# Two blocks of the residual stream kept turned for the queries, and a gate's sums moved into the first FFN

## The chip, the cores and the metric

The kernel runs on one core of one Trainium2 chip. The metric is the time of one execution on the device, in microseconds (us). The engines are named as in the profile: PE (TensorE, matrix products and transposes; PEld its weight loads), DVE (VectorE), ACT (ScalarE), POOL (GpSimd) and SP (SyncE, which here only issues DMAs). Each engine works through its own queue in order; a queue's order is fixed when the program is built.

## What is computed

A decoder trunk of two layers on 256 tokens of width 2048, in float32. Layer 0 mixes by causal pooling, layer 1 by latent attention with 16 heads; each layer ends in a SwiGLU FFN of width 5632. Shifts, scales and gates come from a vector c (`sc = silu(c)`).

```python
for i in range(DEPTH):
    shift_m, scale_m, gate_m, shift_f, scale_f, gate_f = jnp.split(sc @ mod_w[i] + mod_b[i], N_MOD, axis=-1)
    if i == N_A:
        kv_shift, kv_scale = jnp.split(sc @ kv_mod_w + kv_mod_b, 2, axis=-1)
        h_kv = modulate(rmsnorm(x, kv_in_norm), kv_shift, kv_scale)
        kv = shared_kv(h_kv, w_dkv, kv_norm, w_uk, w_uv, w_kr, cos, sin)
    h = modulate(rmsnorm(x, norm_mix[i]), shift_m, scale_m)
    if i < N_A:
        y = pool_mixer(h, pool_w[i], pool_scale[i])
    else:
        j = i - N_A
        y = mla_mixer(h, kv, w_dq[j], q_norm[j], w_uq[j], w_o[j], cos, sin)
    x = x + gate_m[:, None, :] * y
    h = modulate(rmsnorm(x, norm_ffn[i]), shift_f, scale_f)
    x = x + gate_f[:, None, :] * swiglu(h, ffn_gate[i], ffn_up[i], ffn_down[i])
return rmsnorm(x, final_norm)
```

The keys and the queries of layer 1 both start from `rmsnorm(x)` of the same x. They differ only in gain, shift and scale per column, so the stream divided by its root mean square and turned (columns to partitions) serves both.

## The kernel before

**Weight units.** Every large product is made of weight units: 512 rows by 512 columns of a weight, 1 MB, loaded by SP into one of six `raw` tiles (`w_unit`, load at L387). ACT rounds it to a high half (L374), DVE subtracts to get the low half (L376), both in tiles `hl` (six, so three units). PE then makes 24 products per unit for the two token tiles (L398): high by high, high by low of the activations, low by high. Activations in halves lie in `act` tiles, eight of 8 KB per partition, which serve many other uses too.

**Background units.** The modulation vectors `sc @ mod_w` are not made on PE, apart from the first ones. Each is a list of units; one unit (`Part.unit`) loads 1 MB of the transposed weight by SP (L210) into a `raw` tile and lets DVE multiply it by `silu(c)` and sum along the row (L211, one instruction that takes the sum along). There are 168, in this order: 24 for the first FFN's shift and scale, 16 for its gate, 32 for the keys' shift and scale, 48 for the attention's shift, scale and gate (`mla`), 32 for the last FFN's shift and scale, 16 for its gate. They are spread by hand: `plan(left, units)` sets a rate so that `left` remain after so many weight units; each `split` of a weight calls `tick`, which issues the units that have come due. `hold` stops this, `release` starts it again with a new rate. In the first FFN the rate is 75 units over 95 weight units, 6 remain for the keys, and 19 lie beside the queries' latent and the heads.

**Stages.** Pooling mixer; first FFN (its first three blocks of 512 columns by `start_ffn`, which pumps eight units in each, then chunks `p`, `t`, `d` in a fixed list); handover into the keys' latent; keys and values (four groups of four heads) with the queries' latent between them; heads in eight pairs; output product with w_o; last FFN; final norm.

**Handover.** `then_attention` runs with its order written by hand on PE, ACT and DVE. While the FFN's last column ends for token tile 0 and then 1, the first two blocks of the stream are scaled (`scale`, L476: block 0 on DVE, block 1 on POOL), turned by PE (`turn`, L482), and made into halves: `upper` (ACT, L490), `whole` (L497 on DVE or L499 on ACT) and `lower` (DVE, L503). Products are L407; `a` is block 0, `b` block 1, the digit the token tile, and the index 0, 1, 2 the group high-high, low-high, high-low. Blocks 2 and 3 follow in a loop: scaled by POOL (L528), turned (L540), halves at L1183 to L1193, products at L1197. Then the rotary key (L1201, L1208) and the latent's norm (L1238 to L1241).

**Queries.** `hidden_q` scales a block again on ACT (`scaled`, L530), turns it with eight transposes (L540), and modulates it (L558 to L560), for each of four blocks.

**Heads.** `project_heads` makes q for a pair (weights split at L1362 and L1363, products L1368 to L1370 and L1288), `probabilities` the softmax (L1383 to L1401), `turned` transposes (L1407), `weighted` the sums over values (L1414, L1415). PSUM has eight banks.

Of the kernel before, what the change touches and what calls it, by code (L numbers as in the profile page):

```python
# [17 lines left out]
P = 128  # L18
# [42 lines left out]
BEGUN = 6  # L61
ASIDE = 5

FFN0_UNITS, MLA_UNITS, HEAD_UNITS, WO_UNITS, FFN1_UNITS = 95, 4, 16, 8, 60

KNOWN = (1, 3, 5, 7, 9, 10, 11, 12)


LATE, MLA_LATE, WO_LATE = 3, 5, 3

V_C, V_NM, V_NF, V_KVIN, V_KVN, V_QN, V_PS, V_B, V_KB, V_END = 0, 16, 48, 80, 96, 100, 104, 120, 312, 344

# [21 lines left out]
def tile_trunk(ctx: ExitStack, tc: tile.TileContext, a: dict, out: bass.AP):  # L94
# [22 lines left out]
    def t2k(shape, dt=F32):  # L117
        return work.tile(shape, dt, tag="t2k", bufs=7, name=nm("t2k"))
# [323 lines left out]
    def run(*lists):  # L442
        for fs in lists:
            for f in fs:
                f()
# [3 lines left out]
    class Handover:  # L449
# [23 lines left out]

        def scale(self, tok, j):
            self.turned[tok, j] = t2k([P, CH]), ps_t().rearrange("p (k t) -> p k t", k=KL), t2k([P, KL, P])
            (dve if j == 0 else pool).tensor_scalar(out=self.turned[tok, j][0], in0=x[:, tok, j * CH:(j + 1) * CH],  # L476
                                                    scalar1=self.rstd[:, tok:tok + 1], scalar2=None, op0=ALU.mult)

        def turn(self, tok, j):
            xr, pt, _ = self.turned[tok, j]  # L480
# [233 lines left out]
    def ffn(l, hT, gate_name, begun, then):  # L714
# [23 lines left out]
        def down(i):  # L738
# [6 lines left out]
            for j in range(ND):  # L745
                js = slice(j * CH, (j + 1) * CH)
                banks = [ps_t() for _ in range(NT)]
                if last and j == ND - 1:
                    hold()
                if last and j == ND - 1:  # L750
                    weights = [w_unit(wd[c, j]) for c in g]
# [118 lines left out]
    def start_ffn(l, first, ahead, hidden, late):  # L870

        begun = begin(l, range(BEGUN), (0,))
        hT = [first(begun[0])] if l == DEPTH - 1 else [first]
        with tc.issue_after(mod_ins[0].ins), tc.issue_after(hid_ins[0].ins) if hid_ins[0] else nullcontext():
            for j in range(ND - 1):
                if l == 0 and j == 1:
                    for tok in range(NT):
                        sync.dma_start(aside[0][:, tok], back[tok])
                todo = KD // 2 if j + 1 >= ND - late else 0
                for n, (c, which) in enumerate((c, w) for c in begun for w in (GATE, UP)):  # L880
                    if n == 2 * len(begun) - 1:
                        hT.append(hidden(j + 1, pieces))
                    if l == 0 or j > 0 or c > 0:
                        begun[c][which].block(j, hT[j])
                    if n == 2 * len(begun) - 5:
                        pieces = ahead(j + 1)
                    if todo:
                        pump(1)
                        todo -= 1
                pump(todo)  # L890
        return hT, begun
# [215 lines left out]
    for j in range(ND):  # L1107
        sf_block(1, j, C_SF1, C_AF1)
    mod_part(1, 5, gate_to, "ffn1")
    n_ffn1, n_blocks, n_mix = KD, KD // 2, KD  # L1110
    n_late = n_ffn1 + LATE * n_blocks
    n_all = n_ffn1 + ND * n_blocks + n_mix

    hT, begun = start_ffn(0, first, hidden_T, lambda j, parts: halves_T(j, parts), ND - 1)
    plan(n_all + MLA_LATE, FFN0_UNITS)

    hkv, rstd, ckv = None, None, []

    def dkv(j):
        return a["w_dkv"][j, 0]  # L1120
# [1 line left out]
    def then_attention(old, banks, piece):  # L1122
# [4 lines left out]
        hkv, rstd = h.hT, h.rstd  # L1127
        w = [w_load_of(dkv(j)) for j in range(2)]
        split_upper(w[0])
        run(h.old(0))  # L1130
        h.start()
        h.piece(0)
# [1 line left out]
        split_upper(w[1])  # L1134
        h.scale(0, 0)
        h.scale(0, 1)
        split_lower(w[0])
        fs = h.old(1)
        run(fs[:-KL])
        h.turn(0, 0)  # L1140
# [22 lines left out]
        h.lower(0, 1)  # L1163
        h.turn(1, 1)
        h.upper(1, 1)
        run(b0[2], a1[2], b1[0], b1[1])
        h.whole(1, 1, dve)
        h.lower(1, 1)
        run(b1[2])

        pieces = [scaled(rstd, j, pool) for j in range(2, ND)]
        for j in range(2, ND):
            w_ = w_load_of(dkv(j))
            if j == 2:
# [3 lines left out]
            split_upper(w_)  # L1178
            t_ = act_t([P, 2, KL, T])
            full = [t2k([P, 2, T]) for _ in range(2)]  # L1180
            columns = [[cols[:, i, j * KL + k:j * KL + k + 1] for i in (C_AKV, C_SKV)] for k in range(KL)]
            for k, (by, plus) in enumerate(columns):
                act.activation(t_[:, 0, k, :], pts[k // 2][:, k % 2, :], AF.Identity, scale=by, bias=plus)  # L1183
            split_lower(w_)
            for k, (by, plus) in enumerate(columns):
                src, dst = pts[k // 2][:, k % 2, :], full[k // 2][:, k % 2, :]
                if k < 2:
                    dve.tensor_scalar(out=dst, in0=src, scalar1=by, scalar2=plus, op0=ALU.mult, op1=ALU.add)
                else:
                    act.activation(dst, src, AF.Identity, scale=by, bias=plus)  # L1190
            for k2 in range(2):
                ks = slice(2 * k2, 2 * k2 + 2)
                dve.tensor_tensor(out=t_[:, 1, ks], in0=full[k2], in1=t_[:, 0, ks].bitcast(F32), op=ALU.subtract)  # L1193
# [103 lines left out]

    def hidden_q():
        nonlocal pieces
        pts = turned_pieces(pieces)  # L1300
        if len(hmx) < ND - 1:
            pieces = scaled(rstd, len(hmx) + 1)
        hmx.append(modulated(pts, len(hmx), C_AM1, C_SM1))

# [10 lines left out]
    pool.memset(krT, 0.0)  # L1315
    rope_end(kr_t, [(slice(0, ROPE), krT[0:ROPE, 0, :]), (slice(ROPE, P), krT[ROPE:P, 1, :])])

    plan(n_all - n_mix - WO_LATE, HEAD_UNITS)
    cq = [ps_t() for _ in range(NT)]
    for j in range(ND):  # L1320
        if len(hmx) < ND:
# [108 lines left out]
    pairs = H // HG  # L1430

    act.activation(small([P, 1]), ones[:, 0:1], AF.Exp)
    hold()
    heads = [project_heads(g) for g in range(2)]
    for o in heads:
        o.finish()
    release(n_all - n_mix - WO_LATE, HEAD_UNITS - 8)

    w_o, ob = a["w_o"], []

# [137 lines left out]
```

## Time and profile before

| | us |
|---|---|
| median of 3 runs | 1918.96 (1916.93 to 1919.68) |
| the profiled execution | 1918.19 |
| its span, first to last instruction | 1916.4 |
| PE busy | 1862.8 (97%) |
| DVE busy | 1402.7 (73%) |
| ACT busy | 850.2 (44%) |
| POOL busy | 26.9 (1%) |
| DMA | 574.98 MB, mean 300 GB/s |

The times of single instructions come from the profiled execution. In the profile's rows a name such as `ps<-hl,act` gives output and inputs without buffer numbers, `x24` a count, and a bracket such as `[0.80 <-POOL t2k L476]` the time for which the engine stood idle just before and the instruction that ended it. The granted clock over the whole span was 0.987 of full speed.

### The profile page before, as it was taken

What the parts mean: (1) busy time and instruction counts of PE and PEld (TensorE: products, weight loads), DVE (VectorE), ACT (ScalarE), POOL (GpSimd) and SP (SyncE); (2) the same over time, 40 slices, a digit from 0 to 9 for tenths busy, and PEclk for the clock granted to TensorE, in tenths of its full rate; (3) what the DMA queues carried; (4) which work ended last, traced back from release to release, by engine and by line L of the source; (5) the groups of instructions that cost most, each with busy time, mean ns of one, the idle gap of its engine ahead of it and who ended that gap; (6) DMA issues with size and microseconds to landing.
All of it is one profiled execution on the core that took longest, in us unless ns stands there. A gap on an engine that the chain in (4) does not pass through costs nothing.

```text
span 1916.4 us, 21930 instructions
## 1 busy us (share of the span) xinstructions
PE 1862.8 (97%) x8813; PEld 1507.8 (79%) x8813; DVE 1402.7 (73%) x1391; ACT 850.2 (44%) x958; POOL 26.9 (1%) x32
## 2 busy tenths in 40 slices
PE   7689999999999999999999999999999999999998
PEld 3255888888888888887889888888888888888887
DVE  2148799999788777799899966889785556645556
ACT  3125643444433334244678745634444433343343
POOL 0000000000000000002100000000000000000000
PEclk9789999999999999999999999999999999999999
DMA  9999998879998888897597775988776666665651
GB/s 399 398 418 417 368 364 333 319 299 361 357 344 332 327 330 326 332 373 274 212 371 291 293 278 194 397 318 335 260 284 240 241 240 239 249 222 205 220 198 44
DMA packets 86647, 574.98 MB, mean 300 GB/s; under 512 B 10977, under 2 KB 15505, under 8 KB 18321
## 3 DMA queue, kind: packets, MB, share of 16 engines
q1 hardware_dynamic: 86018, 570.42, 77.8%
q0 software_dynamic: 432, 3.15, 0.4%
q8 instruction: 69, 1.13, 0.2%
q14 instruction: 32, 0.26, 0.0%
q10 hardware_dynamic: 96, 0.02, 0.0%
HBM read 567.24 MB, written 6.32 MB: 299 GB/s over the span
## 4 chain that ended last, share of the span: by engine, by line
PE 69%; issue 22%; DMA 3%; DVE 3%; ACT 1%; SPq 0%; POOL 0%; POOLq 0%; DVEq 0%; ACTq 0%
PE ps L398 58%; DMA raw<-in_mod_w_dram 3%; PE ps L256 2%; PE ps L973 2%; PE ps L407 2%; PE ps L1288 2%; DVE raw L211 1%; PE ps L729 1%; PE ps L1197 1%; PE ps L540 0%; DMA raw<-in_mod_block_dram 0%; PE ps L196 0%; PE ps L948 0%; PE ps L770 0%; DVE hl L376 0%
## 5 line engine op out<-in xcount | busy, mean ns | idle before, releaser
L398 PE MATMUL ps<-hl,act 128*128 128x512 f32 x6744 | 1539.5, 390 | 1.9 <-DVE hl L376 1.0
L398 PEld LDWEIGHTS ps<-hl,act 128*128 128x128 f32 x6744 | 1263.0, 188 | 264.7 <-DVE hl L376 1.8
L376 DVE TENSOR_TENSOR hl<-raw,hl 128x2048 fp32r<-128x2048 f32 x289 | 661.1, 2289 | 253.2 <-ACT hl L374 252.5
L374 ACT ACTIVATE hl<-raw 128x2048 fp32r<-128x2048 f32 x289 | 553.1, 1918 | 647.8 <-PE ps L398 572.1
L211 DVE SCALAR_TENSOR_TENSOR raw<-raw,s_row 128x2048 f32<-128x2048 f32 x168 | 383.2, 2284 | 3.6 <-DMA raw<-in_mod_wt_dram 3.6
L256 PE MATMUL ps<-raw,s_strip 128*32 128x512 f32 x392 | 65.2, 760 | 34.6 <-DMA raw<-in_mod_w_dram 33.5
L698 DVE TENSOR_TENSOR act<-ps,act 128x512 f32<-128x512 f32 x96 | 64.5, 685 | 17.5 <-PE ps L398 17.5
L256 PEld LDWEIGHTS ps<-raw,s_strip 128*32 128x32 f32 x392 | 9.5, 121 | 70.0 <-DMA raw<-in_mod_w_dram 46.3
L784 DVE TENSOR_TENSOR x<-ps,x 128x512 f32<-128x512 f32 x32 | 22.1, 690 | 38.8 <-PE ps L398 38.8
L1288 PE MATMUL ps<-act,hl 128*128 128x256 f32 x384 | 49.6, 287 | 0.0
L1288 PEld LDWEIGHTS ps<-act,hl 128*128 128x128 f32 x384 | 48.3, 195 | 0.7 <-DVE act L1253 0.2
L407 PE MATMUL ps<-hl,act 128*128 128x512 f32 x192 | 47.0, 400 | 1.2 <-DVE act L503 1.2
L732 ACT ACTIVATE act<-ps 128x512 fp32r<-128x512 f32 x44 | 23.6, 594 | 50.0 <-PE ps L729 37.6
L407 PEld LDWEIGHTS ps<-hl,act 128*128 128x128 f32 x192 | 35.2, 188 | 10.7 <-ACT act L490 2.3
L263 DVE COPY t2k<-ps 128x256 f32<-128x256 f32 x4 | 1.7, 425 | 52.9 <-ACT t2k L262 52.9
L427 ACT ACTIVATE junk<-x 128x512 bf16<-128x512 f32 x23 | 14.5, 629 | 53.2 <-DVE x L612 37.6
L802 DVE TENSOR_TENSOR t2k<-ps,t2k 128x512 f32<-128x512 f32 x24 | 16.5, 689 | 28.5 <-PE ps L398 28.5
L798 ACT ACTIVATE t2k<-ps 128x512 f32<-128x512 f32 x24 | 14.2, 590 | 47.9 <-PE ps L398 47.9
L973 PEld LDWEIGHTS ps<-act,act 128*128 128x128 f32 x128 | 24.7, 200 | 11.6 <-issue 8.4
L696 ACT ACTIVATE act<-ps 128x512 f32<-128x512 f32 x32 | 19.1, 597 | 29.0 <-PE ps L398 28.8
L973 PE MATMUL ps<-act,act 128*128 128x256 f32 x128 | 31.9, 402 | 0.0
L733 DVE TENSOR_TENSOR act<-ps,act 128x512 fp32r<-128x512 f32 x44 | 28.1, 683 | 0.9 <-ACT act L732 0.9
(222 smaller groups left out, 911.6 us busy)
## 6 DMA issues: line engine op xcount, KB each, us to landing
raw<-in_mod_wt_dram SPq DMA_DIRECT2D x136, 1024.0 KB, 5.8
raw<-in_ffn_gate_dram SPq DMA_DIRECT2D x88, 1024.0 KB, 5.8
raw<-in_ffn_up_dram SPq DMA_DIRECT2D x88, 1024.0 KB, 5.1
raw<-in_ffn_down_dram SPq DMA_DIRECT2D x88, 1024.0 KB, 5.2
raw<-in_mod_w_dram SPq DMA_DIRECT2D x48, 1024.0 KB, 12.1
raw<-in_kv_mod_wt_dram SPq DMA_DIRECT2D x32, 1024.0 KB, 7.1
raw<-in_w_o_dram SPq DMA_DIRECT2D x16, 1024.0 KB, 6.1
raw<-in_mod_block_dram SPq DMA_DIRECT2D x8, 1024.0 KB, 12.5
```

What stands on the lines that cost most here:

```text
L211: dve.scalar_tensor_tensor(out=r, in0=r, scalar=1.0, in1=s_row, op0=ALU.mult, op1=ALU.mult, accum_out=self.sums[:, self.n:self.n + 1])
L256: pe.matmul(self.bank[m * STRIP:(m + 1) * STRIP, :], lhsT=weights(k), rhs=r[:, k, i, :], start=first, stop=last)
L374: hi_ins = act.activation(hi, r, AF.Copy)
L376: lo_ins = dve.tensor_tensor(out=lo, in0=r, in1=hi.bitcast(F32), op=ALU.subtract)
L398: pe.matmul(banks[tok], lhsT=t_[:, i, k, tok * P:(tok + 1) * P], rhs=w[:, k, :], start=first and n < len(part), stop=last and n >= len(ord ...
L407: pe.matmul(bank, lhsT=t_[:, i, k, tok * P:(tok + 1) * P], rhs=w[:, k, :], start=first and n == 0, stop=last and n == len(order) - 1)
L698: dve.tensor_tensor(out=part, in0=banks[tok], in1=part, op=ALU.add)
L732: act.activation(m[:, 0, :, ts_], v, AF.Copy)
L733: dve.tensor_tensor(out=m[:, 1, :, ts_], in0=v, in1=m[:, 0, :, ts_].bitcast(F32), op=ALU.subtract)
L784: dve.tensor_tensor(out=x[:, tok, js], in0=banks[tok], in1=x[:, tok, js], op=ALU.add)
L973: pe.matmul(mixed[g][:, n % 2, :], lhsT=wp[g][:, k, ns], rhs=pool_all[g // 2][:, g % 2, k, :], start=k == 0, stop=k == KL - 1)
L1288: pe.matmul(pt[:, h, :], lhsT=w(h0 + h, k), rhs=t_[:, i, k, :], start=n == 0, stop=n == 3 * KL - 1)
```

## The change

Four things are moved:

1. *Kept blocks.* In the keys' latent, blocks 2 and 3 of the stream, turned and not yet modulated, are copied by ACT out of PSUM into a float32 tile of the `act` kind (two copies of 128x512 per block). `hidden_q` takes them from there for its blocks 2 and 3 and no longer scales and turns them.
2. *The gate's units.* `n_mix` goes out of the counts: the 16 units of `mla`'s gate come due before the heads. The first FFN's rate becomes 91 units over 94 weight units. The plans and the hold and release around the heads go; the output product takes eight units over nine weight units in place of five over eight. In the last group of an FFN's down product `hold` comes one column of 512 earlier, which leaves seven units for the keys.
3. *Handover.* `scale` is always on DVE; the low half of the first weight is subtracted ahead of the old products; `a1[2]` goes ahead of `b0[2]`.
4. *Start of an FFN.* In its first block the eight units start at the third weight unit and not at the first.

```diff
-FFN0_UNITS, MLA_UNITS, HEAD_UNITS, WO_UNITS, FFN1_UNITS = 95, 4, 16, 8, 60
+FFN0_UNITS, MLA_UNITS, WO_UNITS, FFN1_UNITS = 94, 4, 9, 60
-LATE, MLA_LATE, WO_LATE = 3, 5, 3
+LATE, MLA_LATE = 3, 5
...
-            (dve if j == 0 else pool).tensor_scalar(out=self.turned[tok, j][0], in0=x[:, tok, j * CH:(j + 1) * CH],
-                                                    scalar1=self.rstd[:, tok:tok + 1], scalar2=None, op0=ALU.mult)
+            dve.tensor_scalar(out=self.turned[tok, j][0], in0=x[:, tok, j * CH:(j + 1) * CH],
+                              scalar1=self.rstd[:, tok:tok + 1], scalar2=None, op0=ALU.mult)
...
-                if last and j == ND - 1:
+                if last and j == ND - 2:
                     hold()
...
-                    if todo:
+                    if todo and (j > 0 or n + 2 >= 2 * len(begun) - todo):
                         pump(1)
...
-    n_ffn1, n_blocks, n_mix = KD, KD // 2, KD
+    n_ffn1, n_blocks = KD, KD // 2
     n_late = n_ffn1 + LATE * n_blocks
-    n_all = n_ffn1 + ND * n_blocks + n_mix
+    n_all = n_ffn1 + ND * n_blocks
...
         split_upper(w[0])
+        split_lower(w[0])
         run(h.old(0))
...
         h.scale(0, 1)
-        split_lower(w[0])
...
-        run(b0[2], a1[2], b1[0], b1[1])
+        run(a1[2], b0[2], b1[0], b1[1])
...
+        mem = act_t([P, 2, KL, T], F32)
+        both = [mem[:, i] for i in range(2)]
...
+            kept.append([both[j - 2][:, 2 * h2:2 * h2 + 2] for h2 in range(2)])
...
+            for pt, dst in zip(pts, kept[-1]):
+                act.activation(dst, pt, AF.Copy)
...
-        pts = turned_pieces(pieces)
-        if len(hmx) < ND - 1:
+        pts = turned_pieces(pieces) if len(hmx) < 2 else kept[len(hmx) - 2]
+        if len(hmx) < 1:
             pieces = scaled(rstd, len(hmx) + 1)
...
-    plan(n_all - n_mix - WO_LATE, HEAD_UNITS)
...
-    hold()
     heads = [project_heads(g) for g in range(2)]
     for o in heads:
         o.finish()
-    release(n_all - n_mix - WO_LATE, HEAD_UNITS - 8)
```

More of the change, by code (lines that the diff above doesn't have):

```diff
@@ L1109, in tile_trunk @@
     mod_part(1, 5, gate_to, "ffn1")
-    n_ffn1, n_blocks, n_mix = KD, KD // 2, KD
+    n_ffn1, n_blocks = KD, KD // 2
     n_late = n_ffn1 + LATE * n_blocks
-    n_all = n_ffn1 + ND * n_blocks + n_mix
+    n_all = n_ffn1 + ND * n_blocks
     hT, begun = start_ffn(0, first, hidden_T, lambda j, parts: halves_T(j, parts), ND - 1)
     plan(n_all + MLA_LATE, FFN0_UNITS)
-    hkv, rstd, ckv = None, None, []
+    hkv, rstd, ckv, kept = None, None, [], []
     def dkv(j):
```

## The prediction

> **What bounds the kernel now.** I read the page first, then stretches of time, then the order of time on single engines where TensorE (PE) waits. In the page's first and fifth parts (line, engine, operation, shapes, count | busy us, mean ns | idle before) the reader is to see that PE is busy 97% of the span, and what one background unit costs on VectorE (DVE): L211, 2284 ns, plus an 83 ns read of its accumulator, together 2.37 us. A weight unit costs DVE 2289 ns (L376).
>
> ```profile
> PE 1862.8 (97%) x8813; PEld 1507.8 (79%) x8813; DVE 1402.7 (73%) x1391; ACT 850.2 (44%) x958; POOL 26.9 (1%) x32
> ...
> L376 DVE TENSOR_TENSOR hl<-raw,hl 128x2048 fp32r<-128x2048 f32 x289 | 661.1, 2289 | 253.2 <-ACT hl L374 252.5
> ...
> L211 DVE SCALAR_TENSOR_TENSOR raw<-raw,s_row 128x2048 f32<-128x2048 f32 x168 | 383.2, 2284 | 3.6 <-DMA raw<-in_mod_wt_dram 3.6
> ```
>
> Busy is not proof of full rate, so I price a matmul by the chain that ended last (start, length, what): 65.08 / 287 = 0.2268 us per 512-column product, 24 of them 5.44 us per weight unit.
>
> ```profile
> 966.98 0.87 PE ps L540 x8
> ...
> 1098.00 65.08 PE ps L398 x287
> ```
>
> Next the stretches (columns: stretch, length, busy time of PE, weight load, DVE, ACT, POOL with counts, PE clock, DMA share, GB/s).
>
> ```profile
> 390.00:885.00 495.00, 494.85 (x2225) 410.44 (x2224) 407.77 (x326) 196.04 (x147) 0.70 (x1) 1.00 0.88 337
> 810.00:890.00 80.00, 79.85 (x361) 66.14 (x360) 74.70 (x68) 33.93 (x31) 0.00 (x0) 1.00 0.91 359
> 810.00:830.00 20.00, 20.00 (x90) 16.56 (x89) 19.30 (x17) 7.91 (x5) 0.00 (x0) 1.00 1.01 420
> ...
> 390.00:450.00 60.00, 60.00 (x274) 49.86 (x273) 59.06 (x58) 27.69 (x27) 0.00 (x0) 1.00 0.78 287
> ...
> 1010.00:1098.00 88.00, 85.59 (x581) 79.18 (x580) 84.76 (x175) 71.31 (x186) 0.61 (x1) 0.98 0.78 286
> 1030.00:1040.00 10.00, 9.19 (x59) 8.99 (x60) 9.12 (x23) 7.79 (x23) 0.00 (x0) 0.83 0.80 289
> 1098.00:1163.00 65.00, 65.00 (x288) 53.79 (x288) 42.85 (x35) 27.40 (x25) 0.00 (x0) 1.00 0.72 270
> ```
>
> The first FFN (390 to 885) holds PE at 494.85 of 495; DVE has 87 us free there, but only 0.94 in 390 to 450 and 5.3 in 810 to 890. In the heads (1010 to 1098) DVE is the fullest, 84.76 of 88. That invites the conclusion that taking units out of the heads gives back their whole DVE time. PE's order of time there says otherwise:
>
> ```profile
> 1010.16 0.28 PE L1368 MATMUL ps<-act,hl 128*128 128x256 f32 x1
> ...
> 1030.81 0.55 PE L1407 MATMUL ps<-con,t2k 128*128 128x128 f32 x3 [1.97 <-ACT t2k L1400]
> 1031.11 0.36 PE L1368 MATMUL ps<-act,hl 128*128 128x256 f32 x1
> ...
> 1033.33 3.81 PE L1288 MATMUL ps<-act,hl 128*128 128x256 f32 x24
> 1036.98 0.60 PE L1414 MATMUL ps<-t2k,act 128*128 128x256 f32 x2
> ...
> 1041.49 0.36 PE L1368 MATMUL ps<-act,hl 128*128 128x256 f32 x1
> ...
> 1043.00 3.04 PE L1288 MATMUL ps<-act,hl 128*128 128x256 f32 x24
> 1045.88 0.60 PE L1414 MATMUL ps<-t2k,act 128*128 128x256 f32 x2
> ```
> ```profile
> 1063.66 0.60 PE L1414 MATMUL ps<-t2k,act 128*128 128x256 f32 x2
> ```
>
> L1414 recurs once for each pair of heads. From 1045.88 to 1063.66 two pairs take 17.78 us, 8.89 each, with PE going from one matmul to the next: PE's own rate. Eight pairs are 71.1 us. From pair 0's first product at 1010.16 to 1163.08, where the products of 1098.00 end, PE also runs the 14 units of w_o that L398 serves, 336 products: 76.2 us. Together 147.3 of 152.9. So PE loses only 5.6 us there, and that is the ceiling of what relief in the heads can give.
>
> **The change part by part.**
> *Heads: no units.* Nineteen units (16 of mla's gate, 3 of the shift and scale sums of the last FFN) leave the latent projections and the heads. What PE lost: 1.97 us idle at 1030.81, and then slow matmuls: the twelve from 1031.11 took 2.22 us against 1.51 at 1041.49, the 24 of L1288 after them 3.65 against 2.88, 1.5 too long together; the clock in 1030 to 1040 is 0.83. The idle time was put down to ACT's L1400, behind a reciprocal that stood behind a unit:
>
> ```profile
> 1027.82 2.29 DVE L211 SCALAR_TENSOR_TENSOR raw<-raw,s_row 128x2048 f32<-128x2048 f32 x1
> ...
> 1030.03 0.16 DVE L1399 RECIPROCAL sm<-sm 128x2 f32<-128x2 f32 x1
> ```
> ```profile
> 1030.35 0.41 ACT L1400 ACTIVATE t2k<-t2k,sm 128x128 f32<-128x128 f32 x1
> ```
>
> Without the unit the reciprocal could run 2.2 us sooner; ACT's own order may keep some of it. Bounds: 0 (work only leaves) and 5.6. I take 3.0: the 1.5 of the slow clock and three quarters of the idle 1.97.
> The Trainium skill, "TensorE: Matmul & The Clock Gate", section "What's actually happening", says that the clock drops after an idle window of about 3.4 us. Here it fell to 0.83 after a gap of 1.97. By that rule the gap would not be the cause and the 1.5 would stay: the sum would end at 1914.1, inside the forecast's own range.
>
> *Kept blocks.* Two sets of eight transposes (0.87 us each, at 966.98 and alike) leave a stretch where PE goes without a gap: 1.7 us, on the path. Bounds 0 and 1.74. ACT also loses four scalings, off the path. It gains four copies of 128x512 out of PSUM in the keys' latent, priced by ACT's like copies:
>
> ```profile
> L696 ACT ACTIVATE act<-ps 128x512 f32<-128x512 f32 x32 | 19.1, 597 | 29.0 <-PE ps L398 28.8
> ```
> ```profile
> 925.09 1.93 ACT L1183 ACTIVATE act<-ps,cols 128x256 fp32r<-128x256 f32 x4 [2.25 <-PE ps L540]
> ...
> 927.79 2.02 ACT L1201 ACTIVATE hl<-raw 128x1024 fp32r<-128x1024 f32 x2
> ...
> 931.29 3.99 PE L1208 MATMUL ps<-act,hl 128*128 128x256 f32 x32
> ```
>
> Two copies are 1.2 us per block. The first pair falls into ACT's 2.25 us of waiting before 925.09. The second runs ahead of wkr's split (L1201), which then ends at 927.79 + 1.2 + 2.02 = 931.0, just before PE takes its result at 931.29; the norm's squares queue behind it. Bounds 0 and 1.2; I take +0.3, near the end that these rows show. The kept tile holds one of eight act buffers, so the fourth block of the queries waits for the first to come free, one weight unit (5.44) after its use starts, and it is wanted two units later still: nothing, and up to 5.4 if ACT's queue stands behind it.
>
> *Handover into the keys' latent.* Scaling of the second block moves from POOL to DVE (0.49 us by DVE's L476 against 3.98), one weight half is subtracted earlier, and a1[2] goes ahead of b0[2].
>
> ```profile
> 894.28 2.29 DVE L211 SCALAR_TENSOR_TENSOR raw<-raw,s_row 128x2048 f32<-128x2048 f32 x1
> ...
> 896.75 0.68 DVE L611 TENSOR_TENSOR x<-ps,gate 128x512 f32<-128x512 f32 x1
> ...
> 899.87 0.49 DVE L476 TENSOR_SCALAR t2k<-x,rstd 128x512 f32<-128x512 f32 x1 [0.69 <-POOL rstd L472]
> 899.93 3.98 POOL L476 TENSOR_SCALAR t2k<-x,rstd 128x512 f32<-128x512 f32 x1
> ...
> 900.41 0.66 PE L482 MATMUL ps<-con,t2k 128*128 128x128 f32 x4 [1.41 <-DVE t2k L476]
> ...
> 903.97 0.66 PE L482 MATMUL ps<-con,t2k 128*128 128x128 f32 x4 [0.80 <-POOL t2k L476]
> ...
> 912.88 4.83 PE L407 MATMUL ps<-hl,act 128*128 128x512 f32 x20 [1.18 <-DVE act L503]
> ```
>
> PE waits 1.41, 0.80 and 1.18 us at the three marked places: bound 3.4. The 0.80 is POOL's and goes. The 1.41 stays: its cause is piece(0) at 896.75 behind the unit of 894.28, and in that place now stands the subtraction moved up, 2.29 against 2.28. Of the 1.18, the new order saves one DVE subtraction, about 0.8. Other bound: the two scalings stand 0.49 us in front of the second half of w[1], a loss of 0.5. I take 1.6.
>
> *Start of the FFNs.* The first two units of block 0 come two weight units later. PE's waits for DVE halves there:
>
> ```profile
> 183.83 5.51 PE L398 MATMUL ps<-hl,act 128*128 128x512 f32 x23 [0.38 <-DVE hl L376]
> ...
> 189.92 5.28 PE L398 MATMUL ps<-hl,act 128*128 128x512 f32 x22 [0.58 <-DVE hl L376]
> ```
>
> 0.38 + 0.58 bound the gain, zero the other side, since the units only move; 0.5. In the last FFN PE runs without a gap there: nothing.
>
> *First FFN: sixteen more units.* Its rate goes from 75/95 to 91/94 of a unit per weight unit, +0.179; holding one column earlier moves two units out of its end into the keys. That is some 15 units, 35.5 us of DVE and 15.7 MB. On the whole they fit: 407.8 + 35.5 of 495, and 337 + 32 GB/s against 420 seen at 810. In 390 to 450, 11 weight units bring 2.0 extra units, 4.7 us, into 0.94 free: 3.7 too many. In 810 to 890, 2.6 units, 6.2 us into 5.3: 0.9 too many. What hides it is the lead of the split weights:
>
> ```profile
> 169.39:435.00 265.61, 262.76 (x1152) 215.70 (x1153) 1.00 0.88 340
> ```
> ```profile
> 169.39:435.00 265.61, 111.00 (x49) 1.00 0.88 340
> ```
> ```profile
> 436.29 2.29 DVE L376 TENSOR_TENSOR hl<-raw,hl 128x2048 fp32r<-128x2048 f32 x1 [0.19 <-ACT hl L374]
> ```
>
> The first row counts L398, the second L376. At 435 PE has done 1152 / 24 = 48 units, and DVE has begun 49 subtractions, with one more made before 169.39; the next begins at 436.29, so the 50th unit's low half is there by then. PE wants it two thirds into its 50th unit, at 435 + 5.44 + 3.63 = 444.1. Lead 7.8 us, more than 3.7. If that lead were gone, the cost would be 4.6 us in these two stretches, 35.5 if no unit were covered. Below zero nothing reaches: PE has no idle time there to give. I take +0.6. Each load of a unit also stands on SP's queue ahead of a weight's; the six raw tiles bound how far.
>
> *Keys.* They take seven units in place of six: 0 if PE's lead covers the one more, 2.4 if not; I take +0.3, since the units behind them in the queries go. The gate's spread moves with them: one small transpose, ACT's copy, POOL's broadcast; POOL's next work comes tens of us later: nothing. *Output product.* Eight units in place of five: 7.1 us into DVE's 22 free in 1098 to 1163: nothing; 7.1 if uncovered.
>
> Sum: -3.0 - 1.7 - 1.6 - 0.5 + 0.3 + 0.6 + 0.3 = -5.6. The profiled execution took 1918.19 (span 1916.4), 0.8 under the median 1918.96: 1912.6.
>
> **The rivals.**
> (a) *The first FFN pays; slower.* Place: DVE's queue in 390 to 885, where a unit now stands before nearly every weight's subtraction. For it: 59.06 of 60 busy. Against: the lead of 7.8 us. It ends on the slower side from 10.8 us, that is 4.6 of 15 units uncovered; with half uncovered, 17.8: 1918.2 - 6.2 + 17.8 = 1929.8.
> (b) *It pays a part*, 5 us, the 4.6 above with the lead used up: 1917.0.
> (c) *The heads give nothing*, since ACT (71.31 of 88) and its order set the gap at 1030.81: 1915.6. For it: the wait names ACT, which has 0.41 us of L1400 to do in a queue of its own.
> (d) *All of PE's losses go*: 5.6 in the heads, 3.4 in the handover, 1.0 at the start, 1.7, no costs: 1906.5. Against: ACT's paces in the handover stay.
>
> **How the numbers follow.** The forecast 0.46 (its own range 1909.5 to 1915), (a) 0.11, (b) 0.14, (c) 0.15, (d) 0.14. 0.2%, 3.8 us, is about what a measurement of this kernel tells from no change: faster lies under 1915.1, slower above 1922.8. Faster: nearly all of the forecast, (d) and a third of (c), 0.63. Same: (b) and the rest of (c), 0.25. Slower: (a) with a little of (b), 0.12. The range 1906.5 to 1918.5 leaves out (a) and the outer part of (d).
>
> **What the changed profile would show.** Heads: no L211 between the queries and the output product, pairs still 8.89 us, no 2 us gap before L1407, clock 1.00 throughout. Kept: sixteen fewer of L540. Handover: no POOL L476. First FFN: DVE above 0.88 busy, PE still full. The prediction is wrong if PE shows waits for L376 between 390 and 885, if the gap in the heads comes back elsewhere, or if ACT's copies delay PE before L1208.

## The result and the profile after

| | before | after |
|---|---|---|
| median, us | 1919.14 (6 runs, 1916.93 to 1919.68) | 1931.21 (6 runs, 1928.31 to 1931.93) |
| ratio to before | | 1.0062, 95% interval 1.0049 to 1.0075 |
| profiled execution, span | 1918.19, 1916.4 | 1931.93, 1930.1 |

The change made the kernel 12.1 us slower; the forecast was 1912.6, 5.6 under the profiled execution. The two profiled executions are 13.7 apart. To see where, I cut each trace at five instructions of PE: the first product of the first FFN, the first transposition of the handover's turned block, the first product of the keys' `head_T`, the first product of the heads, and the first transposition of the second handover. The last two columns belong to experiments below.

| stage, us | before | after | plan alone | the rest alone |
|---|---|---|---|---|
| up to the first FFN | 169.39 | 170.15 | 170.61 | 170.07 |
| first FFN, to the first turned block | 731.02 | 739.21 | 738.54 | 734.90 |
| of it PE's wait in front of that block | 1.41 | 0 | 0 | 3.63 |
| handover into the keys' latent, and latent | 37.54 | 36.70 | 36.68 | 38.00 |
| keys and queries | 72.21 | 76.74 | 79.35 | 69.80 |
| heads and output product | 162.73 | 163.83 | 162.36 | 163.09 |
| the rest, to PE's last group | 728.21 | 728.15 | 728.14 | 728.16 |

So 8.2 us (9.6 without the wait of 1.41, which went) were lost in the first FFN and 4.5 in keys and queries; the handover gave 0.8; the heads, which were to give 3.0, cost 1.1.

Lines and stretches of the changed kernel (columns as before; L373, L375, L210, L397 are the former L374, L376, L211, L398):

```profile
PE 1868.2 (97%) x8797; PEld 1509.5 (78%) x8797; DVE 1406.3 (73%) x1393; ACT 849.5 (44%) x958; POOL 18.9 (1%) x30
...
L375 DVE TENSOR_TENSOR hl<-raw,hl 128x2048 fp32r<-128x2048 f32 x289 | 660.7, 2288 | 250.8 <-ACT hl L373 250.6
...
L210 DVE SCALAR_TENSOR_TENSOR raw<-raw,s_row 128x2048 f32<-128x2048 f32 x168 | 383.1, 2283 | 3.7 <-DMA raw<-in_mod_wt_dram 3.7
```
```profile
390.00:885.00 495.00, 490.62 (x2198) 403.88 (x2197) 434.19 (x352) 191.95 (x140) 0.70 (x1) 1.00 0.94 367
810.00:890.00 80.00, 77.65 (x347) 63.12 (x346) 75.54 (x70) 29.88 (x26) 0.00 (x0) 1.00 0.97 389
390.00:450.00 60.00, 60.00 (x279) 49.92 (x278) 59.31 (x59) 27.24 (x24) 0.00 (x0) 1.00 0.82 303
970.00:985.00 15.00, 11.30 (x68) 10.87 (x69) 10.83 (x12) 9.55 (x12) 0.61 (x1) 0.77 1.01 416
1022.00:1110.00 88.00, 84.76 (x574) 78.16 (x572) 65.27 (x153) 70.67 (x184) 0.00 (x0) 0.98 0.48 172
1090.00:1100.00 10.00, 10.00 (x44) 8.63 (x45) 8.18 (x26) 5.64 (x21) 0.00 (x0) 0.83 0.58 210
```

One unit costs what it did (2283 and 2288 ns). In 390 to 885 DVE rose from 407.77 to 434.19, the DMA share from 0.88 to 0.94, and PE, which had been full, lost 4.4 us. In 810 to 890 it lost 2.3 of 80, but in 390 to 450, where the forecast saw the tightest place, nothing. The heads' DVE time fell from 84.76 of 88 to 65.27, and PE was not fuller for it: 84.76 against 85.59.

What the FFN waits for is read from ACT's waits between 200 and 900 (engine, line, releaser: total us, times, longest). Of before:

```profile
ACT hl L374 <- PE ps L398: 204.5, 67, 4.4
...
ACT hl L374 <- DMA raw<-in_ffn_gate_dram: 28.6, 7, 12.1
```

Of after:

```profile
ACT hl L373 <- DMA raw<-in_ffn_down_dram: 80.7, 21, 6.7
ACT hl L373 <- PE ps L397: 65.8, 23, 4.6
ACT hl L373 <- DMA raw<-in_ffn_gate_dram: 54.5, 16, 4.7
```

Before, ACT's split of the next weights mostly waited for PE to free a tile: 204.5 us, the lead in full. After, it waits for the loads: 80.7 and 54.5 us. PE's own waits in the same stretch, and the chain that ended last at one such place:

```profile
PE ps L397 <- ACT hl L373: 4.0, 8, 0.8
PE ps L397 <- DVE hl L375: 1.0, 1, 1.0
```
```profile
484.60 0.02 ACT x L781
...
485.10 1.91 ACT hl L373
...
487.06 5.79 PE ps L397 x24
```

The split (1.91) stands in ACT's queue behind ACT's copy of a finished column (L781), which itself waits for PE; PE stands idle until the split ends. A late load did not hold this split: its load had landed 4.57 us before it started. What differs from before is the order in which ACT's queue was built. Counted from the first weight unit, 57 splits stand ahead of this copy, and PE had begun 56.7 units when the copy ran; before, 59 stand ahead of the same copy, with 56.5 begun.

PE has nine waits for split weights in 200 to 900, 5.0 us together. Eight are for ACT's split. Six of these splits, this one among them, stand right behind ACT's read of a finished column (L781, or L797 in the gate's product), for which ACT waited 2.5 to 10.9 us, and their loads had landed 2.7 to 7.7 us before they started. Of the other two, one load had landed 0.1 us before, so there the load may have been late, and for one the trace has no landing. The 24 products behind the wait shown took 5.79, not 5.44; if the others cost the same 0.35, an estimate from this one, that is 3.2 more, together 8.2.

In the keys, PE's order of time has one gap, and DVE's says why:

```profile
957.74 5.92 PE L1293 MATMUL ps<-act,hl 128*128 128x256 f32 x48
...
973.70 0.37 PE L291 MATMUL ps<-con,cols 128*16 128x128 f32 x1 [4.58 <-DVE cols L299]
973.82 7.98 PE L1293 MATMUL ps<-act,hl 128*128 128x256 f32 x48
```
```profile
966.42 2.28 DVE L375 TENSOR_TENSOR hl<-raw,hl 128x2048 fp32r<-128x2048 f32 x1
968.63 2.28 DVE L210 SCALAR_TENSOR_TENSOR raw<-raw,s_row 128x2048 f32<-128x2048 f32 x1
...
970.84 2.28 DVE L210 SCALAR_TENSOR_TENSOR raw<-raw,s_row 128x2048 f32<-128x2048 f32 x1
...
973.39 0.16 DVE L299 TENSOR_TENSOR cols<-sums,vcol 128x16 f32<-128x16 f32 x1
```

The gate's columns (L299) stand behind two units and w_uv's subtraction, and the small transposition that needs them stands in PE's queue ahead of the 48 products of `head_T`. PE idles 4.58 us, the clock falls (0.77 in 970 to 985), and the 48 products take 7.98 in place of 5.92.

In the heads the early gap of 1.97 is gone and the pairs run from 1022.8 to 1077 without one. Then:

```profile
1078.05 0.55 PE L1411 MATMUL ps<-con,t2k 128*128 128x128 f32 x3 [0.99 <-ACT t2k L1404]
...
1089.55 0.87 PE L1411 MATMUL ps<-con,t2k 128*128 128x128 f32 x3 [2.00 <-ACT t2k L1404]
```
```profile
1086.69 2.29 DVE L375 TENSOR_TENSOR hl<-raw,hl 128x2048 fp32r<-128x2048 f32 x1 [0.67 <-ACT hl L373]
1088.90 0.16 DVE L1403 RECIPROCAL sm<-sm 128x2 f32<-128x2 f32 x1
```

With one of 0.15 between them, 3.14 us, more than the 2.40 of before. In front of the last reciprocal stands now not a unit but w_o's own subtraction, 2.29 again; a clock of 0.83 follows the gap of 2.00, as it followed the gap of 1.97 before.

### The profile page after: what moved, and what is told of

Same layout as the page of the kernel before. It is cut to its first block, busy times and chain, and to the rows that moved or that the text cites. A ratio compares the mean times of both kernels' runs of the same rounds, so it can differ in the third digit from the quotient of the medians.

```text
span 1930.1 us, 21954 instructions
## 1 busy us (share of the span) xinstructions
PE 1868.2 (97%) x8797; PEld 1509.5 (78%) x8797; DVE 1406.3 (73%) x1393; ACT 849.5 (44%) x958; POOL 18.9 (1%) x30
## 4 chain that ended last, share of the span: by engine, by line
PE 87%; DVE 5%; DMA 3%; ACT 3%; issue 1%; SPq 0%; POOL 0%; POOLq 0%; DVEq 0%; ACTq 0%
PE ps L397 76%; DMA raw<-in_mod_w_dram 3%; PE ps L255 2%; PE ps L972 2%; PE ps L406 2%; DVE hl L375 1%; DVE raw L210 1%; ACT hl L373 1%; PE ps L1293 1%; PE ps L728 1%; DMA raw<-in_mod_block_dram 0%; PE ps L195 0%; PE ps L947 0%; PE ps L769 0%; ACT t2k L844 0%
## 5 line engine op out<-in xcount | busy, mean ns | idle before, releaser
L397 PE MATMUL ps<-hl,act 128*128 128x512 f32 x6744 | 1545.2, 390 | 6.2 <-ACT hl L373 4.2
L397 PEld LDWEIGHTS ps<-hl,act 128*128 128x128 f32 x6744 | 1264.4, 188 | 272.5 <-ACT hl L373 8.5
L375 DVE TENSOR_TENSOR hl<-raw,hl 128x2048 fp32r<-128x2048 f32 x289 | 660.7, 2288 | 250.8 <-ACT hl L373 250.6
L373 ACT ACTIVATE hl<-raw 128x2048 fp32r<-128x2048 f32 x289 | 552.7, 1917 | 620.5 <-PE ps L397 434.6
L210 DVE SCALAR_TENSOR_TENSOR raw<-raw,s_row 128x2048 f32<-128x2048 f32 x168 | 383.1, 2283 | 3.7 <-DMA raw<-in_mod_wt_dram 3.7
L797 ACT ACTIVATE t2k<-ps 128x512 f32<-128x512 f32 x24 | 14.2, 590 | 56.3 <-PE ps L397 56.3
```

Of the source, the lines that this page charges most:

```text
L210: dve.scalar_tensor_tensor(out=r, in0=r, scalar=1.0, in1=s_row, op0=ALU.mult, op1=ALU.mult, accum_out=self.sums[:, self.n:self.n + 1])
L373: hi_ins = act.activation(hi, r, AF.Copy)
L375: lo_ins = dve.tensor_tensor(out=lo, in0=r, in1=hi.bitcast(F32), op=ALU.subtract)
L397: pe.matmul(banks[tok], lhsT=t_[:, i, k, tok * P:(tok + 1) * P], rhs=w[:, k, :], start=first and n < len(part), stop=last and n >= len(ord ...
```

## The experiments

"Before" stands for the runs of the unchanged kernel on the same chip, 1917.8 to 1918.9 in the four sets.

**The plan alone, and the rest alone.**

```diff
# e1_budget, in the kernel before
-FFN0_UNITS, MLA_UNITS, HEAD_UNITS, WO_UNITS = 95, 4, 16, 8
+FFN0_UNITS, MLA_UNITS, WO_UNITS = 94, 4, 9     # n_mix gone, hold() at ND - 2,
-    plan(n_all - n_mix - WO_LATE, HEAD_UNITS)  # no hold/release in the heads
# e2_rest: the changed kernel with these lines as before
```

> The kernel before with the new unit plan alone (first FFN 94, no unit in the query projections and heads, output product 9, hold one column earlier); kept blocks, handover and start as before. Theory 1, the plan carries the whole loss: the first FFN ends about 9.7 us later, the gate's spread waits on DVE in the keys for about 4.6 us with a slow clock of 2 us after it, the heads give nothing; without the 4 us that the other parts save the time is 1919.1 + 9.7 + 6.2 + 1.0 - 0 = about 1935 (1931 to 1939). Rival, the loss comes from the kept blocks (ACT's four copies, the act buffer held through the queries) or from their meeting the plan: 1925 or less.

> The changed kernel with the old unit plan (16 units in the queries and heads, 95/8, hold in the last column): kept blocks, handover and start of the FFN alone. Theory 1: these save 1.7 (transposes) and 0.8 to 2.2 (handover), with 0 to 0.5 at the start, and cost nothing: 1919.1 - 3.5 = 1915.6 (1914 to 1917). Rival: ACT's copies and the buffer held cost what the transposes save, 1918 or more; no loss from them means that the keys' delay in the changed kernel is the spread's alone.

The plan alone: 1932.86, ratio 1.0075 (95% interval 1.0061 to 1.0088; so for every run below), 15 us slower. It carries the whole loss, in the same two stages. The rest alone: 1920.20, 1.0013 (1.0004 to 1.0021): no gain, 2.4 slower. Keys and queries are 2.4 us shorter there, so the kept blocks work, and the new gap in that stage is the plan's. But PE waits 3.63 in front of the first turned block. DVE's order, with the subtraction moved up (L519):

```profile
896.64 2.28 DVE L210 SCALAR_TENSOR_TENSOR raw<-raw,s_row 128x2048 f32<-128x2048 f32 x1
...
898.85 2.29 DVE L519 TENSOR_TENSOR hl<-raw,hl 128x2048 fp32r<-128x2048 f32 x1
...
901.32 0.68 DVE L610 TENSOR_TENSOR x<-ps,gate 128x512 f32<-128x512 f32 x1
...
904.43 0.88 DVE L475 TENSOR_SCALAR t2k<-x,rstd 128x512 f32<-128x512 f32 x2 [0.69 <-POOL rstd L471]
```
It stands behind the unit, not in its place: 2.28 + 2.29 in front of the residual sum (L610) on which the norm waits.

**DVE's part or the loads' part of the units.** A unit is a load of 1 MB and 2.37 us of DVE. Two kernels took away either part of every sixth unit; a third added the loads alone to the kernel before.

```diff
# e3_dve, every sixth unit of the first FFN:  cs = slice(0, CH)
+dve.scalar_tensor_tensor(out=r[:, cs], in0=r[:, cs], in1=s_row[:, cs], ...)
# e4_dma, the same units:
+sync.dma_start(r[:, :CH], self.w[row:row + P, :CH])   # and DVE 4 times over it
# e5_loads, the kernel before, at every third weight unit of the first FFN:
+sync.dma_start(spare, a["mod_wt"][0, row:row + P, :2 * CH])
```

> The changed kernel, but in the first FFN every sixth background unit has DVE multiply and sum only 512 of its 2048 columns (its load stays whole), so those sums are not the reference's. DVE's work there falls by 15 units of 1.7 us, 26 us, to about the level of the kernel before; the bytes loaded stay at the new level. Theory A, DVE's queue sets the pace: the first FFN gives back 7 to 10 us, time 1921 to 1924, and PE's waits for the split weights go. Theory B, the six raw tiles, which DVE frees late: also a gain, 4 to 8 us. Theory C, the loads (0.94 DMA share): no change, 1930 to 1932.

> The changed kernel, but in the first FFN every sixth unit loads only 512 of its 2048 columns (256 KB in place of 1 MB) and DVE works through them four times, so those sums are not the reference's. Bytes fall by 15 x 0.75 MB, 11.8 MB, to about the level of the kernel before; DVE's time stays (four pieces of a quarter, about 0.3 us more per such unit, 4.5 in all). Theory A, DVE's queue: no gain, 1931 to 1935. Theory B, the raw tiles: a small gain, since such a tile is filled sooner, 0 to 4 us. Theory C, the loads: 7 to 10 us less, 1921 to 1924.

> The kernel before, with its own plan, and in the first FFN 31 more loads of 512 KB (15.9 MB in all, as many bytes as the new plan adds there) into a spare tile that nothing reads: no work for DVE, none of the six raw tiles. Theory C, the loads' bandwidth: the first FFN loses what it lost with the new plan, 6 to 8 us, time 1924 to 1926, with PE waiting for ACT's split and ACT for loads. Theory B, the six raw tiles (or A, DVE): the spare loads take none, 1918 to 1919.

Less DVE work: 1930.28, 1.0063 (1.0051 to 1.0076), the first FFN 739.05. Nothing came back, though DVE had been relieved by more than 20 us there (595.30 in place of 615.95 in 200 to 900). Theory A, that DVE's time sets the pace, falls. Fewer bytes: 1930.64, 1.0069 (1.0057 to 1.0082), but the stage shows what the total hides: 737.85, of which 3.32 is a new wait in front of the turned block, so 4.7 us came back in the products and DVE was late next. But 4.9 of the 9.6 stayed lost, with 239.71 MB in 200 to 900, 3.0 more than before. Loads alone, without a unit more: 1927.52, 1.0053 (1.0041 to 1.0065), and the first FFN is 740.05, with no wait in front of the block:

```profile
ACT hl L376 <- PE ps L406: 82.9, 29, 4.4
...
ACT hl L376 <- DMA raw<-in_ffn_down_dram: 53.0, 13, 6.0
ACT hl L376 <- DMA raw<-in_ffn_gate_dram: 46.1, 11, 10.9
```
```profile
PE ps L406 <- ACT hl L376: 3.8, 5, 2.0
PE ps L406 <- DVE hl L378: 2.4, 2, 1.8
```

Same signature: the lead (82.9 in place of 204.5) becomes waiting for loads. These loads hold none of the six raw tiles and no DVE time, so neither is needed for a loss of this size. Bytes in 200 to 900, of before, after and the loads alone:

```profile
DMA packets 34484, 236.67 MB, mean 338 GB/s; under 512 B 5668, under 2 KB 5684, under 8 KB 5684
```
```profile
DMA packets 36507, 251.39 MB, mean 359 GB/s; under 512 B 5896, under 2 KB 5912, under 8 KB 5912
```
```profile
DMA packets 36889, 251.57 MB, mean 359 GB/s; under 512 B 4145, under 2 KB 4161, under 8 KB 8257
```

14.7 and 14.9 MB more. That looks like theory C. But putting more loads into the program also changed the order in which ACT's queue was built. The table shows it at one place, the eight copies of a finished column in the first group of the down product (L782 before, L781 after). It counts the splits that stand ahead of each, from the first weight unit on:

| kernel | splits ahead of the eight copies |
|---|---|
| before, the rest alone | 53, 54, 56, 57, 59, 59, 62, 62 |
| fewer bytes | 53, 53, 55, 56, 58, 59, 61, 61 |
| loads alone | 52, 53, 54, 55, 57, 58, 61, 61 |
| after, plan alone, less DVE work | 52, 52, 54, 55, 57, 58, 60, 61 |

With the order of before, PE waits for no split between 200 and 900; with fewer splits ahead it does, and the three kernels with the last order wait at the same first eight places. In the loads alone PE waited five times for ACT's split, and each time that split's load had landed 7.9 us or more before the split began, and ACT had just read a finished column or block out of PSUM for which it had waited for PE (5.8 to 14.2 us). So at these places PE did not stand for late bytes but for a split queued behind such a read. Whether later loads would cost anything in the order of before, and what in the build moves the splits back, no run here shows. The same holds for the six raw tiles (B): between 200 and 900 SyncE's queue waited 541 us before and 547 us after for DVE to free one, so they set when a load starts in either kernel.

**The gate's spread in the keys.**

```diff
# e6_spread, the changed kernel
-            pending.append((0, spread))
+            put_off.append(spread) if name == "mla" else pending.append((0, spread))
     ...
+    put_off.pop()()                   # behind the queries' last product
     end, cqT = Latent(cq, V_QN), []
```

> The changed kernel, but the spread of the gate named mla (one small transpose on PE, ACT's copy, the broadcast) is issued after the queries' last product instead of in the keys. Theory: PE's 4.6 to 5.2 us of waiting before that transpose and the slow clock after it (2 us) go, keys to heads falls from 76.7 to about 70 (69.8 without the units there), time 1931.2 - 6.5 = 1924.7 (1923.5 to 1927). Rival: DVE's seven units in the keys delay PE anyway, the wait moves to the next subtraction there, 1929 to 1932.

1923.35, 1.0026 (1.0016 to 1.0036): 7.9 us less than the changed kernel by the medians. Keys and queries take 69.89 in place of 76.74, 6.85 less: 4.58 of waiting and 2.06 of slow clock. The transposition now runs at 1001.82 without a wait.

**The useful parts together, and alone.**

```diff
# e7_best, the kernel before with the kept blocks, hold() at ND - 2 and the later start
# e9_kept, the kernel before with the kept blocks alone
# e10_handover: e9_kept and
-            (dve if j == 0 else pool).tensor_scalar(out=self.turned[tok, j][0], ...)
+            dve.tensor_scalar(out=self.turned[tok, j][0], ...)
-        run(b0[2], a1[2], b1[0], b1[1])
+        run(a1[2], b0[2], b1[0], b1[1])
# e12_start, the kernel before with the later start alone
```

> The kernel before with three parts of the change: kept blocks, the plan held one column earlier, the first two units of the FFN later; the old plan's counts and the old handover. From the stages so far: kept blocks -2.4, the hold -1.4 and -0.9 at the handover, the start -0.5, together -5.2: 1912.6 (1911 to 1915). Rival: the two units that the hold moves into the keys cost there what the hold saves, 1915 to 1917.

> The kernel before with the kept blocks alone. From the stages of the run with kept blocks, handover and start together (keys to heads 69.8 against 72.2, heads to the last handover 163.1 against 162.7): -2.4 and up to +0.4, so 2.0 to 2.4 us less, 1916.5 on 1918.7 (1915.5 to 1917.5). Rival: ACT's four copies come back in the heads as later gaps and nothing is left, 1918 or more.

> The kernel before with the kept blocks, and of the handover the second block's scaling on DVE and a1[2] ahead of b0[2], but the subtraction of w[0] left where it was. Theory: of the handover's three edits the subtraction moved up is the one that costs (the turn waited 3.63 in place of 1.41, behind a unit and that subtraction), the others give POOL's 0.8 and part of the 1.18: handover stage (first turn to keys) 37.5 to about 36.2, turn's wait 1.4 to 1.5, time 1.3 under the kept blocks alone, 1915. Rival: the two scalings in front of the subtraction hold back the second block's halves, stage 37.5 or more.

> The kernel before with the start of the first FFN alone: its first two units two weight units later. Theory of the forecast: DVE's two waits there (0.38 and 0.58) go, 0.5 to 1.0 less, 1918. Rival: the slow clock lasts as long as in the six kernels with this edit (0.50 to 0.67 for the first 7 to 8 us, 3.3 us lost by 200) where the four without it lost 0.7 to 3.0, so 0.5 to 1.5 more, 1919.5 to 1920.5.

e7_best missed: 1921.88, 1.0020 (1.0010 to 1.0029). The hold did what it was to do at the handover (first FFN and handover 767.7 together, 768.6 before), but the units that it moves on stand in front of the queries' norm and the first pair: keys and queries 75.06, with these waits at their end:

```profile
999.09 5.06 PE L1293 MATMUL ps<-act,hl 128*128 128x256 f32 x40 [0.89 <-DVE sm L1244]
...
1012.28 0.39 PE L1373 MATMUL ps<-act,hl 128*128 128x256 f32 x1 [1.99 <-DVE hl L1368]
```

Kept blocks alone: 1917.85, 0.9997 (0.9988 to 1.0006). Keys and queries 69.80, 2.4 less than before, and 163.17 in the heads, with 3.9 us of gaps in place of 2.4. That is 0.4 more than in the first profile of before, but 1.9 more than in the second (161.29, next section), which like this one has no slow clock there. With the two handover edits: 1917.73, 0.9993 (0.9984 to 1.0002); handover and latent 37.18 against 37.63, since POOL's 0.8 went and 0.9 of waiting for a half of w[1] (DVE L519) came. The later start: 1919.49, 1.0003 (0.9995 to 1.0012), no change that can be told; the interval leaves room for the rival's 0.5 to 1.5. The profiles speak for it: by the 118th product of the first FFN, PE had lost 3.1 to 3.8 us against 0.2268 a product in the nine profiles with this edit, and 1.8 to 3.0 in the seven without. With it, PE also waits 0.21 to 0.51 for ACT's split at the fifth product.

**A second profile of before.**

> The kernel before once more, for a second profile of it. Whether the slow clock at the first products of the first FFN (0.66 to 0.69 from 170 to 180 in all five changed kernels, 1.00 in the one profile of before) belongs to the kernel or to the execution: if to the execution, the same kernel can show it here, and it is about 2 us of the difference between the profiles; if to the change, the clock is 1.00 here again.

It took 1915.05. The first two rows are of the first profile, the others of this one:

```profile
168.00:172.00 4.00, 3.04 (x15) 2.20 (x16) 2.75 (x9) 3.26 (x5) 0.00 (x0) 1.00 1.02 422
172.00:176.00 4.00, 4.00 (x19) 3.27 (x18) 3.96 (x6) 0.93 (x2) 0.00 (x0) 1.00 1.00 412
```
```profile
168.00:172.00 4.00, 4.00 (x13) 3.11 (x13) 3.86 (x9) 2.89 (x4) 0.00 (x0) 0.64 1.02 418
172.00:176.00 4.00, 4.00 (x19) 3.33 (x18) 4.00 (x5) 1.92 (x1) 0.00 (x0) 1.00 1.01 418
```

The slow clock appears in an unchanged kernel, and so it does in every other profile of this study. So whether it comes is a matter of the execution; how long it lasts may go with the later start (above). Its share in the comparison is small: from its first product to 200.0 before makes 127 products in 30.61 us, the changed kernel 118 in 29.85; at 0.2268 each, 1.8 and 3.1 us are lost there, so 1.3 of the first FFN's 9.6 lies in this start: 2.0 more for slow products and 0.7 less of waits (0.22 in place of 0.38 and 0.58). About as much (1.6) separates the difference of the two traces from that of the medians. The Trainium skill, "TensorE: Matmul & The Clock Gate", section "What's actually happening", has the clock decided by a window that runs freely, not from the kernel's start, so that the same kernel is slow for a varying time; these two profiles agree.

The second profile differs in the heads too:

```profile
1029.08 0.55 PE L1407 MATMUL ps<-con,t2k 128*128 128x128 f32 x3 [1.98 <-ACT t2k L1400]
```
```profile
1028.00:1048.00 20.00, 18.92 (x142) 1.00 0.79 272
```

The gap of the first pair is there again, but the clock stays at 1.00 behind it, and the heads take 161.29, 1.4 less than in the first profile. So the slow clock there, too, belongs to the execution and not to the unit, and heads can be compared only where both profiles have it or both lack it.

**The heads' last pairs.**

```diff
# e11_wo_behind: e6_spread, and
     plan(n_late, WO_UNITS)
+    behind.append(out_ins[0].ins)      # the heads' last subtraction
# e13_split_late: e11_wo_behind, and for w_o's first three units (load as it was)
+            with tc.issue_after(prob_ins[0].ins):   # last scaling of pair 6 of 0 to 7
+                hi, lo = split(r, [P, KL, CH])
# e14_kept_split: e10_handover with the same split
```

> The changed kernel with the gate's spread put off as before, and the output product's eight units held behind the heads' last subtraction (they were moved up into the heads' last third). Theory 1, these units set the late gaps (1.15 and 2.00 before the turned probabilities): gaps go, heads to the last handover 162.2 to about 159, time 1923.4 - 3 = 1920.4. Theory 2, the w_o splits of ACT (1.9 each) and DVE (2.29) that stand there set them: gaps stay, 162 or more, and the units bunched behind cost up to 2 more, 1923 to 1925.

> As the run with the output product's units held behind the heads (spread put off too), and w_o's first three splits (ACT 1.9, DVE 2.29 each) are issued behind the second reciprocal of the last pair but one; their loads stay. Theory: of the 3.2 us of gaps the 2.00 (and the 0.16) are w_o's subtraction standing right in front of a reciprocal; they shrink to under 1, the 1.0 of the pair before it stays, heads to the last handover 162.2 to 163.9 becomes 160.5 to 161.5, time 1923.2 - 2 = 1921. Rival: the splits are then late for their own products, PE waits 2 to 4 us for them behind the last scores, stage 163 to 166.

> The kernel before with the kept blocks and the two cheap handover edits (DVE scaling, order), and w_o's first three splits issued behind the second reciprocal of the last pair but one. In its own heads the gaps were 1.99, 0.45, 0.19 and 1.30, of which the last two stand by w_o's subtractions. Theory: 1 to 1.5 us less in the heads (163.2 to about 162), time 1917.7 - 1.2 = 1916.5, which would be faster than before by about 0.07%. Rival: PE waits for w_o's halves instead, 1918 to 1920.

Without a unit in sight of the heads: 1923.18, 1.0026 (1.0017 to 1.0035), the same as with them, and the gaps did not move (1.01 and 2.00, with 0.16 between):

```profile
1072.65 0.55 PE L1412 MATMUL ps<-con,t2k 128*128 128x128 f32 x3 [1.01 <-ACT t2k L1405]
...
1084.14 0.87 PE L1412 MATMUL ps<-con,t2k 128*128 128x128 f32 x3 [2.00 <-ACT t2k L1405]
```
```profile
1081.29 2.29 DVE L375 TENSOR_TENSOR hl<-raw,hl 128x2048 fp32r<-128x2048 f32 x1 [0.67 <-ACT hl L373]
1083.49 0.16 DVE L1404 RECIPROCAL sm<-sm 128x2 f32<-128x2 f32 x1
```

With w_o's splits taken away too, those three gaps go, and one of 2.82 comes:

```profile
1080.74 0.70 PE L1421 MATMUL ps<-t2k,act 128*128 128x256 f32 x2 [2.82 <-ACT t2k L1416]
```
```profile
1079.34 0.40 ACT L1403 ACTIVATE t2k<-t2k,sm 128x128 f32<-128x128 f32 x1 [1.46 <-DVE sm L1400]
...
1080.23 0.47 ACT L1416 ACTIVATE t2k<-ps 128x384 f32<-128x384 f32 x1
```

Here ACT's copy of the turned probabilities (L1416) stands behind the next head's exponentials, with no unit and no weight split near. Heads and output product take 161.13, 1.1 less than in e6_spread (162.19); the total, 1922.57 or 1.0025 (1.0016 to 1.0035), can't tell. In the kernel with units in its heads: 1917.01, 0.9993 (0.9984 to 1.0001). That is the fastest median of the changed kernels, and not told apart from before.

## Why the prediction was wrong, step by step

- *First FFN, +0.6: the step that failed most.* 9.6 us were lost in place of 0.6, some 8.3 without what its start lost. The forecast priced a unit by its DVE time, and rested its cover on the split weights' lead at 435. That DVE place (390 to 450) lost nothing, thinner DVE work gave nothing back, and between 390 and 885 PE's waits were all for ACT's split, none for DVE's subtraction (L375). The lead of 7.8 us was right for the kernel before, but the forecast took it over for the changed kernel. There it is gone: ACT's queue was built with one or two splits fewer ahead of its reads of a finished column, and PE ran out of split weights nine times. The loads had one sentence: 337 + 32 GB/s against 420 seen at 810. But the 420 came from a stretch whose DMA share was already 1.01, and over the whole FFN the share was 0.88 at 337 GB/s; 32 more at that rate of work is a share of about 0.96, an estimate. More loads are enough for such a loss (8.6 us by the loads alone); whether through their time on the queue or through the new order stays open. Rival (a) had the sign (slower, decided from 10.8 us) and a stage like it, but DVE's queue as its mechanism; that its 1929.8 lies near 1931.2 is luck.
- *Keys, +0.3, and "the gate's spread: nothing".* It cost 6.85: 4.58 of waiting and 2.06 of slow clock. The forecast named POOL's next work and not what stands behind the transposition in PE's queue, nor that the sums it waits for come after seven units on DVE.
- *Heads, -3.0.* Nothing was gained. Without a slow clock, plan alone and the spread put off take 162.36 and 162.19 where before takes 161.29; with it, the changed kernel takes 163.83 where before takes 162.73: 0.9 to 1.1 more. Half of the 3.0 was the slow clock's 1.5, which the unchanged kernel shows in one execution and not in the other. The early gap went as forecast, and others came in the last pairs, first by w_o's subtraction in the unit's place, then by ACT's order. The ceiling of 5.6 was right as arithmetic; that anything under it could be had by taking DVE work out was not. (DVE was not the fullest engine there, as the forecast has it: its own row has PE at 85.59 and DVE at 84.76.) In its result this is rival (c), to which I gave 0.15. Its reason, that ACT set the gap at 1030.81, did not hold, since that gap went with the units; ACT's order sets the last one.
- *Handover, -1.6.* 0.8 to 2.2 came, for another reason. The plan alone and the loads alone, with none of the handover's edits, have handover and latent in 36.68 and 36.78; the edits without the plan make PE's wait 3.63 in place of 1.41. The forecast let the moved subtraction take the unit's place on DVE; with units still there it stood behind one.
- *Kept blocks, -1.7, and ACT's copies, +0.3.* Right in their stage (-2.4), and the copies cost nothing: two take 1.11 us, and PE's wait at the latent's product stays 0.22. But 1.9 of the 2.4 came back in the heads (163.17 against 161.29, both without a slow clock), as gaps whose cause no run shows, and alone they change nothing that can be measured.
- *Start, -0.5.* DVE's waits of 0.38 and 0.58 went, one of 0.5 for ACT's split came, and the time did not measurably change: a ratio of 1.0003 with 1 inside the interval. The longer slow clock of the profiles with this edit speaks against a gain.
- *Output product, 0.* Right: its units cost nothing, in the heads or behind them.

## What to carry to other kernels

Before a lead is taken over from one kernel to another, count it again in the order that the new kernel was built with: here, how many splits stand ahead of each read of a finished column on ACT's queue. A load that has landed does not help while its split stands behind an instruction that waits for PE. Price background work by every queue that it uses, and the transfers by their busy share in the fullest stretch: the best GB/s on the page came from a stretch at full share. Look, for everything that is moved, at what stands behind it on an in-order queue: one small transposition waiting for DVE's backlog cost more than all the transpositions saved. Before two profiles of a stage are compared, see whether both had the slow clock there. Where taking work off an engine is to close a gap, ask what the scheduler will put into that place; here it was the same length of work each time.

## What the runs showed of the hardware

- With 32 more loads of 512 KB, which nothing reads, the kernel became 8.6 us slower with PE at 97%. The DMA share went from 0.88 to 0.92 and the rate from 338 to 359 GB/s in 200 to 900, well under the 420 that single stretches reach. That the bytes themselves cost this is not shown, since the order of ACT's queue changed with them.
- After a gap of 1.97 to 2.00 us in the heads, PE's clock fell in seven of fourteen profiles and stayed at 1.00 in the other seven. The unchanged kernel did both: 0.83 in 1030 to 1040 of the first profile, 1.00 in 1028 to 1048 of the second. After the gap of 4.58 us in the keys it was 0.77 in 970 to 985.
- At the start of the first FFN the clock fell to 0.50 for some microseconds in the changed kernel, where PE had been busy 7.48 of the 10 us before 170 and the last gap was 0.96. In the first profile of before, with 7.14 of 10 us busy and a gap of 0.95, it stayed at 1.00.
